# Four instead of three column groups of an input projection begin with the first half of their rows

## The chip, the cores and the metric

One core of one Trainium2 chip runs the whole program in one launch. The metric is the device time of that launch in microseconds (us), and lower is better. The engines are named as the profile names them: PE (TensorE, the matrix products; PEld is its weight load), DVE (VectorE), ACT (ScalarE), POOL (GpSimd) and SP (SyncE, which here issues the large loads).

## What is computed

Two transformer blocks over 256 tokens of width 2048, in float32. What matters here is the first half of the first block, and the keys and values of the second block's memory attention, which need nothing of the first block and are computed ahead.

```python
def first_block(x, c, w_ada, b_ada, norm1_w, w_in, ...):
    cond = jax.nn.silu(c)
    mod = cond @ w_ada[i] + b_ada[i]                      # 12288 columns
    shift1, scale1, gate1, shift2, scale2, gate2 = jnp.split(mod, N_MOD, axis=-1)
    h = _modulate(_rms(x, norm1_w[i]), shift1, scale1)
    proj = h @ w_in[i]                                    # 2048 x 4096
    u, q, k, v = jnp.split(proj, splits, axis=-1)
    y_ssm = _s5_mixer(u, ...)                             # a state-space scan, then gelu and a gate (w_glu)
    y_att = _dilated_attention(q, k, v, q_norm_w[i], k_norm_w[i])
    mixed = jnp.concatenate([y_ssm, y_att], axis=-1) @ w_out[i]
    x = x + gate1[:, None, :] * mixed
    ...
# of the second block, over the memory mem:
    k = (mem_n @ w_k)
    v = (mem_n @ w_v)
```

## The kernel before

**Weight tiles.** Every large product runs over weight tiles of 512 rows and 512 columns (1 MB), loaded by SP into six buffers `r` in the order of one list, `W`. A tile of kind "w" is split by `split_half` in two halves of 256 rows, each into a rounded part `h` (ACT, line 207) and a rest `l` (DVE, line 208), and `mm3` multiplies them on PE in three passes (lines 221, 222 and 226) into a PSUM tile `g` of two banks for the 256 tokens. There are four buffers for the halves, so ACT and DVE can be two tiles ahead of PE. A tile of kind "a" carries 128 x 2048 of `w_ada`; it meets no product, DVE sums it against `cond` in one instruction (line 964), eight such sums make half of one of the six modulation vectors.

**Column groups.** `group` takes the tiles of one group of 512 columns, one per block of 512 rows, and hands the finished PSUM tile to a function (`done_u`, `done_q`, `done_k`, `done_v`). The input projection `w_in` has eight groups: u0, u1, q2, q3, k4, k5, v6, v7. A group in the list `EARLY` is taken in two parts: rows 0 to 1023 first, whose sum `hold` copies to SBUF by ACT (line 891), and later rows 1024 to 2047, after which `tok` adds the held sum on DVE (line 887) where otherwise it would copy by ACT.

**Order.** Below, w0, w1, ... are the "w" tiles in the order of the list. Stage A is w0 to w37: 16 tiles for the memory's keys, 16 for its values, and the first halves of u0, u1 and q2 (w32 to w37), with 32 ada tiles spread among them by `mixed`, which leaves the last tiles of a stage without. These 32 sums give shift1 and scale1: the first 16 of them the columns of row blocks 0 and 1, the rest those of 2 and 3, without which the second halves can't start. Stage B is w38 to w83: the second halves of u0, u1 and q2 (w38 to w43), then k4 (w44 to w47), v6, v7, q3, k5 (to w63), `w_out` row block 2 (w64 to w67), `w_glu` (w68 to w71), `w_out` row blocks 3 (w72 to w75) and 0 and 1 (w76 to w83), with 48 ada tiles spread among all but the last three.

**What runs beside.** Everything else is a set of Python generators that advance by one step for each "w" tile (`Flow.step`): the state-space sections (`Ssm.prep` and `Ssm.run`, eight sections, mostly DVE, which start when u0 is there), the attention heads (`head1`, in two sets of four), the gate vectors. Each engine then executes its instructions strictly in the order in which they were emitted. Where a product needs an input that isn't there yet, `Flow.until` advances the generators without a tile between: `w_glu` needs `glu_acts`, that is all eight sections, and `w_out` row block 3 needs heads 4 to 7 (the lists `mixed_acts`).

The 43 or 40 buffers of the class constant `NU` are SBUF buffers of 2 KB in each partition for all these intermediates.

Of the kernel before, what the change touches and what calls it, by code (L numbers as in the profile page):

```python
# [148 lines left out]


class Core:
    NU = 40
    NU2 = 15
    NR, NW = 6, 4

# [26 lines left out]
    def unit(self, shape=(128, 512), dtype=F32):  # L182
        return self.up.tile(list(shape), dtype, name=self.nm("u"), tag="u", bufs=self.NU)

# [257 lines left out]
class Ssm:  # L442
# [18 lines left out]
    def params(self):  # L461
# [5 lines left out]
        tmp = lambda: k.small(32)  # L467
        wide = lambda: k.up.tile([128, NA * 32], F32, name=k.nm("q"), tag="u", bufs=k.NU)

# [302 lines left out]
def build(ctx, tc, A, out):  # L772
    nc = tc.nc
    V, S, G, PE, SY = nc.vector, nc.scalar, nc.gpsimd, nc.tensor, nc.sync
    ctx.enter_context(tc.manual_schedule())
    k = Core(ctx, tc)
# [22 lines left out]
    def tiles(name, g, kbs):  # L799
        return [("w", A[name][g, kb]) for kb in kbs]  # L800

    def ada_tiles(*halves):
        return [("a", A["w_ada"][h, kb]) for h in halves for kb in range(8)]

    def mixed(ws, as_, lag=0, lead=0):

        n, m = len(ws) - lag - lead, len(as_)
        j = 0
        for i, w in enumerate(ws):
            W.append(w)  # L810
            while j < m and j * n < (i + 1 - lead) * m:
                W.append(as_[j])
                j += 1
        W.extend(as_[j:])

    R4 = range(4)
    EARLY = (("u", 0), ("u", 1), ("q", 2), )
    ADA = (8, 9, 6, 4, 5, 7)
    LATE = (("k", 4), ("v", 6), ("v", 7), ("q", 3), ("k", 5), )
    mixed(sum([tiles("w_xk", g, R4) for g in R4] + [tiles("w_xv", g, R4) for g in R4]  # L820
              + [tiles("w_in", g, (0, 1)) for _, g in EARLY], []), ada_tiles(2, 0, 3, 1), 3, LEAD)
    mixed(sum([tiles("w_in", g, (2, 3)) for _, g in EARLY]
              + [tiles("w_in", g, R4) for _, g in LATE], [])
          + sum([tiles("w_out", g, (2,)) for g in R4], [])
# [37 lines left out]
    def group(acts, done, kbs, key=None, first=True, last=True, half=None):  # L862


        ps = open_ps.pop(key) if not first else [k.pm(), k.pm()] if half else k.pg()
        for i, kb in enumerate(kbs):
            parts = yield
            fl.until(lambda: kb in acts)
            end = last and i == len(kbs) - 1
            for ts in ((0,), (1,)) if half and end else ((0, 1),):  # L870
                for j in range(2):
                    k.mm3(ps, acts[kb][2 * j:2 * j + 2], parts[j], first and i == 0 and j == 0,
                          end and j == 1, ts)
                if half and end:
                    half(ps[ts[0]], ts[0])
        if half:
            return
        if last:
            fl.add(done(ps))
        else:  # L880
            open_ps[key] = ps
# [151 lines left out]
    def hold(g):  # L1033
        def done(ps):
            held[g] = tok(ps)
            yield
        return done
# [518 lines left out]
    def main():  # L1556
# [14 lines left out]
        done = {"u": done_u, "q": done_q, "k": done_k, "v": done_v}  # L1571
        for n, g in EARLY:
            yield from group(acts1, hold((n, g % 2)), (0, 1))
        for n, g in EARLY:
            yield from group(acts1, done[n](g % 2), (2, 3))
        for n, g in LATE:
            yield from group(acts1, done[n](g % 2), R4)
# [77 lines left out]
```

## Time and profile before

| | us |
|---|---|
| median of three runs | 2687.2 |
| lowest and highest run | 2685.88, 2689.08 |
| the profiled execution | 2691.46 |
| its span in the trace | 2689.7 |
| busy in the span: PE, DVE, ACT, POOL | 2609.1, 1663.0, 1270.9, 101.0 |

The page divides the span into 40 slices of 67 us. The part up to about 650 us, the first ten, is stage A, stage B and a little more. There the slices of DVE read 7997999987 and those of PE 8899998988; behind it PE reads 9 in every slice but the last and DVE 4 to 7. A reader finds in the timeline of an engine the rows in order of time, with the wait before an instruction in brackets and what ended it; tiles can be counted there by line 208, two instructions for each.

### The profile page before, as it was taken

How to read it: one execution, taken by the hardware profiler on the slowest of the kernel's cores; microseconds unless marked ns; L12 is line 12 of the kernel's file. 1: busy time of each engine (PE TensorE's matmuls, PEld its weight loads, DVE VectorE, ACT ScalarE, POOL GpSimd, SP SyncE). 2: the span in 40 equal slices, each digit the busy share in tenths (PEclk: the TensorE clock that was granted, in tenths of full speed). 3: DMA queues.
4: the chain of work that ended last, by engine and by line, in shares of the span. 5: the costliest groups of instructions: out<-in, count | busy, mean ns of one | idle time of the engine just before them, and what ended most of it. 6: DMA issues, size and time to landing. Idle time of an engine off the chain costs nothing.

```text
span 2689.7 us, 31097 instructions
## 1 busy us (share of the span) xinstructions
PE 2609.1 (97%) x12144; PEld 2164.5 (80%) x12144; DVE 1663.0 (62%) x2016; ACT 1270.9 (47%) x1818; POOL 101.0 (4%) x107
## 2 busy tenths in 40 slices
PE   8899998988999999999999999999999999999998
PEld 6678777867888888888888788888888888888887
DVE  7997999987766544554565445655554554554444
ACT  5366456654544344434455555555544434443443
POOL 3000000100000000000000111000000000000001
PEclk9999999998999999999999999999999999999999
DMA  9988765776766555555446434455555555555552
GB/s 356 352 328 319 304 235 216 287 281 231 289 266 238 193 198 188 192 199 188 184 152 219 153 130 171 165 196 184 179 205 194 188 192 188 188 188 191 188 201 94
DMA packets 90147, 578.98 MB, mean 215 GB/s; under 512 B 10000, under 2 KB 12432, under 8 KB 22672
## 3 DMA queue, kind: packets, MB, share of 16 engines
q1 hardware_dynamic: 80928, 561.61, 56.2%
q10 hardware_dynamic: 9072, 15.38, 1.7%
q8 instruction: 95, 1.56, 0.2%
q14 instruction: 52, 0.43, 0.0%
HBM read 570.67 MB, written 6.29 MB: 215 GB/s over the span
## 4 chain that ended last, share of the span: by engine, by line
PE 80%; DVE 14%; ACT 3%; issue 2%; DMA 1%; POOL 0%; ACTq 0%; DVEq 0%; POOLq 0%
PE g L226 25%; PE g L221 25%; PE g L222 24%; DVE l L208 4%; DVE r L964 4%; PE m L238 2%; DVE v L645 1%; ACT h L207 1%; PE m L345 0%; PE m L1504 0%; PE m L1491 0%; PE m L240 0%; DVE C L653 0%; DMA r<-in_w_ada_dram 0%; PE m L226 0%
## 5 line engine op out<-in xcount | busy, mean ns | idle before, releaser
L208 DVE TENSOR_TENSOR l<-r,h 128x1024 fp32r<-128x1024 f32 x866 | 1028.5, 1223 | 569.4 <-ACT h L207 564.4
L221 PE MATMUL g<-h,u 128*128 128x512 f32 x3424 | 1352.5, 395 | 8.2 <-ACT h L207 5.0
L222 PE MATMUL g<-h,u 128*128 128x512 f32 x3424 | 1336.6, 390 | 0.0
L207 ACT ACTIVATE h<-r 128x1024 fp32r<-128x1024 f32 x866 | 883.7, 1056 | 613.7 <-PE g L222 574.5
L226 PE MATMUL g<-l,u 128*128 128x512 f32 x3424 | 920.9, 391 | 34.8 <-DVE l L208 34.8
L226 PEld LDWEIGHTS g<-l,u 128*128 128x128 f32 x3424 | 641.6, 188 | 181.0 <-DVE l L208 49.2
L221 PEld LDWEIGHTS g<-h,u 128*128 128x128 f32 x3424 | 646.7, 189 | 146.0 <-ACT h L207 9.2
L222 PEld LDWEIGHTS g<-h,u 128*128 128x128 f32 x3424 | 646.7, 189 | 132.6 <-issue 1.9
L964 DVE CUSTOM_DVE_ANT_0 r<-r,cond,vec 128x2048 f32<-128x2048 f32 x96 | 224.5, 2343 | 0.2
L274 ACT ACTIVATE u<-m 128x512 fp32r<-128x512 f32 (+1 forms) x80 | 42.8, 575 | 162.4 <-PE m L238 130.9
L294 ACT ACTIVATE j<-u 128x512 bf16<-128x512 f32 (+2 forms) x92 | 47.3, 514 | 120.5 <-DVE u L1224 33.2
L275 DVE TENSOR_TENSOR u<-m,u 128x512 fp32r<-128x512 f32 (+1 forms) x80 | 50.0, 659 | 80.5 <-ACT u L274 80.4
L277 ACT ACTIVATE u<-m,vec 128x256 fp32r<-128x256 f32 x86 | 38.9, 472 | 69.8 <-PE m L345 30.8
L278 DVE SCALAR_TENSOR_TENSOR u<-m,vec,u 128x256 fp32r<-128x256 f32 x86 | 40.0, 481 | 46.5 <-ACT u L277 46.5
L238 PE MATMUL m<-ident,u 128*128 128x128 f32 x372 | 51.7, 283 | 13.1 <-DMA u<-in_mem_dram 8.8
L238 PEld LDWEIGHTS m<-ident,u 128*128 128x128 f32 x372 | 44.9, 146 | 19.8 <-issue 9.4
L302 POOL TENSOR_TENSOR r<-s,mhalf 128x2 f32<-128x2 f32 x5 | 5.5, 1103 | 1084.3 <-DVE s L301 1084.3
L1255 DVE SCALAR_TENSOR_TENSOR w<-g,r,w 128x512 f32<-128x512 f32 x22 | 15.5, 747 | 44.4 <-PE g L226 44.4
L1271 DVE TENSOR_TENSOR w<-g,w 128x512 f32<-128x512 f32 x24 | 16.5, 688 | 40.8 <-PE g L226 40.8
L1527 DVE TENSOR_TENSOR u<-g,u 128x512 f32<-128x512 f32 x22 | 14.2, 686 | 44.3 <-PE g L226 44.3
L1253 DVE TENSOR_TENSOR w<-g,w 128x512 f32<-128x512 f32 x22 | 14.2, 686 | 44.3 <-PE g L226 44.3
L1247 ACT ACTIVATE w<-g,r 128x512 f32<-128x512 f32 x22 | 13.9, 686 | 52.9 <-PE g L226 52.9
(244 smaller groups left out, 1198.0 us busy)
## 6 DMA issues: line engine op xcount, KB each, us to landing
r<-in_w_ada_dram SPq DMA_DIRECT2D x96, 1024.0 KB, 5.7
r<-in_wg_dram SPq DMA_DIRECT2D x88, 1024.0 KB, 4.8
r<-in_wu_dram SPq DMA_DIRECT2D x88, 1024.0 KB, 4.8
r<-in_wd_dram SPq DMA_DIRECT2D x88, 1024.0 KB, 4.8
r<-in_w_in_dram SPq DMA_DIRECT2D x32, 1024.0 KB, 5.8
r<-in_w_out_dram SPq DMA_DIRECT2D x32, 1024.0 KB, 4.9
r<-in_w_qkv_dram SPq DMA_DIRECT2D x24, 1024.0 KB, 4.8
r<-in_w_xk_dram SPq DMA_DIRECT2D x16, 1024.0 KB, 8.0
```

The source lines that it names most:

```text
L207: nc.scalar.activation(h, r, AF.Copy)
L208: (nc.gpsimd if shared else nc.vector).tensor_tensor(l, r, h.bitcast(F32), op=OP.subtract)
L221: nc.tensor.matmul(ps[t][:, :n], al[:, s], h[:, k], start=first and k == 0, stop=False)
L222: nc.tensor.matmul(ps[t][:, :n], ah[:, s], h[:, k], start=False, stop=False)
L226: nc.tensor.matmul(ps[t][:, :n], ah[:, s], l[:, k], start=False, stop=last and k == len(acts) - 1)
L238: self.nc.tensor.transpose(o, i, self.ident)
L274: nc.scalar.activation(h, ps, AF.Copy)
L275: nc.vector.tensor_tensor(l, ps, h.bitcast(F32), op=OP.subtract)
L277: nc.scalar.activation(h, ps, AF.Copy, scale=w)
L278: nc.vector.scalar_tensor_tensor(l, ps, w, h.bitcast(F32), op0=OP.mult, op1=OP.subtract)
L294: self.nc.scalar.activation(j[:, :n], src, AF.Square, accum_out=acc)
L964: V.tensor_tensor_reduce(r, r, cond, 1.0, v("b_ada", 8 * h + j), OP.mult, OP.add, md[h // 2][:, n:n + 1])
```

## The change

```diff
 class Core:
-    NU = 40
+    NU = 43
...
-    EARLY = (("u", 0), ("u", 1), ("q", 2), )
+    EARLY = (("u", 0), ("u", 1), ("q", 2), ("k", 4))
     ADA = (8, 9, 6, 4, 5, 7)
-    LATE = (("k", 4), ("v", 6), ("v", 7), ("q", 3), ("k", 5), )
+    LATE = (("v", 6), ("v", 7), ("q", 3), ("k", 5), )
...
-    nc = bacc.Bacc("TRN2", target_bir_lowering=False, num_devices=1, dynamic_dma_scratch_size=512)
+    nc = bacc.Bacc("TRN2", target_bir_lowering=False, num_devices=1, dynamic_dma_scratch_size=128)
```

The group k4 joins `EARLY`. Its first two tiles become w38 and w39, the last of stage A, and their sum is held in SBUF; the second halves of u0, u1, q2 and k4 follow as w40 to w47. From w48 on every weight tile has its old place. Stage A has 40 tiles instead of 38 for the same 32 ada tiles, stage B 44 instead of 46 for 48. Three buffers are added to the 40 and the reserve for DMA descriptors shrinks, to make room for the held sum.

In the following excerpts of the engines' orders, `l`, `h` and `r` are the parts and the load of a weight tile, `g` and `m` PSUM tiles, `u` intermediates; a line of "..." marks rows that are left out.

DVE, from tile w34 on, before: the last sum of stage A (L964) stands just above this, and L267 finishes the modulated input of row block 2.

```order
L208 TENSOR_TENSOR l_2144<-r_2057,h_2143 128x1024
L208 TENSOR_TENSOR l_2148<-r_2057,h_2147 128x1024
L208 TENSOR_TENSOR l_2183<-r_2060,h_2182 128x1024
...
L208 TENSOR_TENSOR l_2217<-r_2099,h_2216 128x1024
...
L267 TENSOR_TENSOR u_2255<-u_2256,u_2254 128x512
```

DVE, from tile w34 on, after:

```order
L208 TENSOR_TENSOR l_2138<-r_2051,h_2137 128x1024
L208 TENSOR_TENSOR l_2142<-r_2051,h_2141 128x1024
L964 ISA r_2054,mod_111<-r_2054,cond,vec 128x2048
...
L208 TENSOR_TENSOR l_2180<-r_2093,h_2179 128x1024
...
L964 ISA r_2096,mod_111<-r_2096,cond,vec 128x2048
...
L208 TENSOR_TENSOR l_2217<-r_2132,h_2216 128x1024
```

The last two sums of stage A moved behind w34 and w35, and L267 comes two tiles later; of the sums, 24 now stand before w28 where it was 26.

PE, between the last tile of `w_out` row block 2 (w67) and the first of `w_glu` (w68), before: eight transposes of the first glu input, eight of the second, and the scores of head 4 (L1105).

```order
L226 MATMUL g_4593<-l_4566,u_3992 128x512 x4
L238 MATMUL m_4646<-ident,u_2542 128x128
...
L238 MATMUL m_4664<-ident,u_3497 128x128
...
L1105 MATMUL m_4682<-u_4543,u_4186 128x128
...
L221 MATMUL g_4645<-h_4613,u_4652 128x512
```

PE, in the same place, after (L757 is the output of the last state-space section, L1105 the scores of a head, L1121 the transposes of head 4, L980 a gate vector):

```order
L226 MATMUL g_4574<-l_4547,u_3933 128x512 x4
L757 MATMUL m_4623<-u_2747,u_4344 128x64
...
L1105 MATMUL m_4638<-u_4524,u_4092 128x128
...
L1105 MATMUL m_4681<-u_4524,u_4092 128x128
...
L238 MATMUL m_4700<-ident,u_2615 128x128
...
L1121 MATMUL m_4736<-ident,u_4644 128x128 x3
L1105 MATMUL m_4745<-u_4531,u_4099 128x128
...
L980 MATMUL m_4760<-u_4653,ones 128x512
L221 MATMUL g_4622<-h_4590,u_4706 128x512
```

The last section's output moved from the place before w66 to this one, and three heads are scored here where it was one: two steps of the generators are run off without a tile between.

PE, between w71 (the last of `w_glu`) and w72 (the first of `w_out` row block 3), before: the outputs of heads 5, 6 and 7 (L1127), with transposes between.

```order
L1127 MATMUL m_4959<-u_4885,u_3709 128x128
...
L1121 MATMUL m_4965<-ident,u_4817 128x128 x3
L1127 MATMUL m_4996<-u_4969,u_3709 128x128
...
L1121 MATMUL m_5004<-ident,u_4896 128x128 x3
L238 MATMUL m_5010<-ident,u_4974 128x128
...
L1127 MATMUL m_5028<-u_5008,u_3709 128x128
...
L221 MATMUL g_4958<-h_4926,u_4878 128x512
```

PE, in the same place, after:

```order
L226 MATMUL g_4862<-l_4894,u_3732 128x512 x4
L1127 MATMUL m_4991<-u_4933,u_3647 128x128
L1128 MATMUL m_4991<-u_4933,u_3647 128x128
L1129 MATMUL m_4991<-u_4933,u_3648 128x128
L221 MATMUL g_4990<-h_4958,u_4793 128x512
```

Only the output of head 7 is left here; the other steps went ahead of w68.

## Rows read from the trace of the kernel before

**Rows 1.** Stretches: us; then PE, PEld, DVE, ACT, POOL busy; granted clock, DMA share, GB/s.

```profile
80.00:100.00 20.00, 16.71 (x75) 13.28 (x76) 19.55 (x59) 6.11 (x8) 0.53 (x1) 1.00 1.00 364
...
220.00:240.00 20.00, 20.00 (x90) 16.55 (x89) 15.21 (x14) 9.97 (x12) 0.00 (x0) 1.00 1.01 426
...
560.00:580.00 20.00, 13.15 (x52) 9.73 (x53) 14.96 (x20) 12.32 (x25) 0.00 (x0) 0.74 0.70 260
```

**Rows 2.** Timeline of PE, w28 to w30: start, duration, instruction, wait and its releaser.

```profile
206.06 1.20 PE L226 MATMUL g<-l,u 128*128 128x512 f32 x4 [0.35 <-DVE l L208]
...
211.63 1.07 PE L226 MATMUL g<-l,u 128*128 128x512 f32 x4
...
217.07 1.07 PE L226 MATMUL g<-l,u 128*128 128x512 f32 x4
```

**Rows 3.** Timeline of DVE: w28, a sum, w29, w33, w35 and w36, w39.

```profile
204.78 2.36 DVE L208 TENSOR_TENSOR l<-r,h 128x1024 fp32r<-128x1024 f32 x2
207.06 2.35 DVE L964 CUSTOM_DVE_ANT_0 r<-r,cond,vec 128x2048 f32<-128x2048 f32 x1
...
209.33 2.36 DVE L208 TENSOR_TENSOR l<-r,h 128x1024 fp32r<-128x1024 f32 x2
...
228.59 2.36 DVE L208 TENSOR_TENSOR l<-r,h 128x1024 fp32r<-128x1024 f32 x2 [1.00 <-ACT h L207]
...
239.28 4.79 DVE L208 TENSOR_TENSOR l<-r,h 128x1024 fp32r<-128x1024 f32 x4 [3.79 <-ACT h L207]
...
269.43 2.35 DVE L208 TENSOR_TENSOR l<-r,h 128x1024 fp32r<-128x1024 f32 x2
```

**Rows 4.** Timeline of DVE: a sum before w26, and the wait before w28.

```profile
190.09 2.35 DVE L964 CUSTOM_DVE_ANT_0 r<-r,cond,vec 128x2048 f32<-128x2048 f32 x1
...
200.00 0.69 DVE L267 TENSOR_TENSOR u<-u,u 128x512 fp32r<-128x512 f32 x1 [0.75 <-ACT u L265]
```

**Rows 5.** Timeline of DVE in stage B, up to w67.

```profile
276.29 1.29 DVE L887 TENSOR_TENSOR u<-g,u 128x512 f32<-128x512 f32 x2
...
288.92 0.69 DVE L739 TENSOR_TENSOR u<-m,u 128x512 f32<-128x512 f32 x1 [1.49 <-PE m L736]
...
493.94 0.69 DVE L739 TENSOR_TENSOR u<-m,u 128x512 f32<-128x512 f32 x1 [1.21 <-PE m L736]
...
508.88 0.68 DVE L750 TENSOR_TENSOR u<-u,u 128x512 f32<-128x512 f32 x1
...
510.88 2.35 DVE L964 CUSTOM_DVE_ANT_0 r<-r,cond,vec 128x2048 f32<-128x2048 f32 x1
...
517.95 2.36 DVE L208 TENSOR_TENSOR l<-r,h 128x1024 fp32r<-128x1024 f32 x2 [0.17 <-ACT h L207]
```

**Rows 6.** Timeline of DVE from w68 to w73: the waits, and the first head.

```profile
527.35 2.48 DVE L275 TENSOR_TENSOR u<-m,u 128x512 fp32r<-128x512 f32 x4 [2.08 <-ACT u L274]
529.75 0.34 DVE L1110 SCALAR_TENSOR_TENSOR u<-m,rq,u 128x128 f32<-128x128 f32 x1
...
535.01 2.36 DVE L208 TENSOR_TENSOR l<-r,h 128x1024 fp32r<-128x1024 f32 x2 [1.48 <-ACT h L207]
...
547.95 1.29 DVE L1183 TENSOR_TENSOR u<-u,u 128x512 f32<-128x512 f32 x2 [3.05 <-ACT u L1182]
...
557.90 1.29 DVE L275 TENSOR_TENSOR u<-m,u 128x512 fp32r<-128x512 f32 x2 [2.29 <-ACT u L274]
...
566.97 1.29 DVE L1183 TENSOR_TENSOR u<-u,u 128x512 f32<-128x512 f32 x2 [2.84 <-ACT u L1182]
...
579.15 1.29 DVE L1205 TENSOR_TENSOR u<-g,u 128x512 f32<-128x512 f32 x2 [2.20 <-PE g L226]
```

**Rows 7.** Timeline of PE between w71 and w72: the waits.

```profile
560.95 0.49 PE L1127 MATMUL m<-u,u 128*128 128x128 f32 x2 [2.82 <-ACT u L1123]
...
564.68 1.09 PE L1121 MATMUL m<-ident,u 128*128 128x128 f32 x3 [2.80 <-ACT u L1117]
...
567.81 2.27 PE L238 MATMUL m<-ident,u 128*128 128x128 f32 x8 [2.04 <-DVE u L1183]
```

## The prediction

> **What bounds the kernel now.** [...]
>
> Read second, the two engines' rows at the end of stage A [rows 2, 3]. PE takes 5.44 us for a weight tile (217.07 less 211.63, both the same block of two tiles in a row). DVE takes 2.27 us for the two `l` halves of a tile and 2.27 us for a sum over an ada tile, 4.55 us for the pair (209.33 less 204.78). While DVE also has the state-space preparation it is the slower one: PE waits for its `l` until w28 (206.06, released by DVE). From w28 PE is the slower one, and at 228.59 and 239.28 DVE waits for an `h` whose buffer PE still holds.
>
> Read third, the waits of DVE before w_glu and w_out [rows 6] and of PE in the same place [rows 7].
>
> **The change part by part.** From w48 on every tile stands where it stood; k4's first two tiles move from w44 and w45 to w38 and w39, and the six tiles of u0, u1 and q2 come two tiles later. The 32 sums of stage A spread over 35 tiles, not 33, the 48 of stage B over 41, not 43.
>
> *Added work.* hold() copies k4's half sum out of PSUM (two copies on ACT), and done_k then adds on DVE where it copied on ACT. ACT has as many copies as before; DVE has two additions more, 1.29 us by the same addition for u (the row of 276.29) [rows 5]. No other engine gains an instruction; the buffers (43) and the scratch change no row. **+1.3 us**.
>
> *End of stage A.* By the order 24 sums stand before w28, not 26. One of the two was taken out early (w14), where DVE decides: 2.27 us gained. The other stood at 190.09 [rows 4]; behind it DVE waits 0.75 us for ACT at 200.00 anyway, and PE's own transposes set the rest, so I count 2.1. At w28 the changed kernel is thus 4.4 us ahead. From there PE sets the pace, and there are two tiles more to the handover: 2 x 5.44 = 10.9 us. The handover, the first tile behind stage B's two leading sums (w39 at 269.43 [rows 3], now w41), comes 10.9 - 4.4 = 6.5 us later, near 275.9. DVE has done two tiles (4 x 1.14 = 4.55 us) more by then and equally many sums (34), so 6.5 - 4.55 = **1.95 us** of the delay is new idle time. Bounds: 1.8 (both sums count in full) to 4.5 (the transfers, below). The tiles and sums moved out of stage B are paid back there, since DVE decides.
>
> *Stage B up to w67.* From 269.43 to 517.95 [rows 3, 5] DVE idles 5.8 us in seven waits (1.49 at 288.92 the first, 0.17 at 517.95 the last) [rows 5]. The state-space sections run two tiles later, all in the same relation to their tiles. I take **0**, with bounds of 4.2 us on either side: the three waits of L739 for PE (1.49 us the first, 1.21 the last, 4.2 in sum) gone, or doubled. One thing stays behind: section 7's last four multiplications (2.00 us, 508.88 to 510.88 [rows 5]) stand after w65 now and after w67 then.
>
> *The forced steps.* w68 needs all eight sections, w72 needs heads 4 to 7, and what is not ready is run off without a tile between. The order shows two such steps of the heads before w72 and none before w68; after the change two before w68 (section 7 is late) and none before w72. Before: from 520 to 580 us DVE idles in six gaps [rows 6], 2.08 + 1.48 + 3.05 + 2.29 + 2.84 + 2.20 = 13.9 us; the last three lie at w72, where PE waits 2.82 + 2.80 + 2.04 [rows 7]. After, walked along the order from the end of w67's `l`, with the durations of the same instructions: DVE reaches head 4 at 7.4, and w69's `l` starts 5.3 us later as it did (529.75 to 535.01), a gap of 2.1; behind head 5 the copies of the glu inputs come on ACT after its exp and four gate copies, a gap of 2.8; DVE then stands before head 4's output, which waits for PE to do all of w68 (5.44 us) and the product, a gap of 5.7 and a small one of 0.4; then one of 2.8 for the sigmoid with its table load. That is 13.8, **-0.1 us**. Bounds: -7.3 if the three gaps at w72 go and nothing new comes (2.29 + 2.84 + 2.20), +7.3 if they come twice.
>
> *Sum.* 1.3 + 1.95 + 0 - 0.1 = +3.1 us. It is made against the profiled execution, 2691.46 us (span 2689.7 and 1.8 around it): 2694.6. That execution is 4.3 us above the median of the runs, 2687.2, and the same difference there gives **2690.3 us**. About 0.2% (5.4 us) is what a measurement of this kernel can tell from no change, so this counts as no change.
>
> **Rivals.** *The forced steps cost more at w_glu than they did at w_out (slower).* For it: before w68 they need DVE, which still has sums and tiles queued ahead of the last section's transposes, and ACT, where the exps and gate copies stand ahead of the glu copies; at w72 they mostly needed ACT and PE; and a longer gap of PE lowers its clock behind it, as in 560 to 580 [rows 1]. Against it: PE has 8 us of small work there to cover them. Price: the gaps at w72 twice, 7.3 us, 2690.3 + 7.3 = 2697.6. In my walk PE idles 11 us between w67 and w68; the rival decides from about 14 (2.4 us more take the sum past 5.4).
>
> *They are covered (faster).* In the kernel before, the glu transposes and a score run between w67 and w68 and DVE waits only 2.08 us. If the new ones hide as well, the gaps at w72 go, and the one for the sigmoid (3.05) too, since heads no longer crowd ACT there: 7.3 + 3.05 = 10.4 us less, 2679.9. Against it: w68 cannot start before a chain over DVE, PE, ACT and DVE again.
>
> *The transfers fall behind at the end of stage A (slower).* From w28 to w35 each tile now has its sum: 16 transfers of 1.05 MB in 8 x 5.44 = 43.5 us, 385 GB/s. The stretch 80 to 100 with DMA fully busy moved 364 GB/s, 220 to 240 moved 426 [rows 1]. At 364 the 16.8 MB take 46.1 us: 2.6 more, 2692.9, just beyond what counts as the same. [...] Hence a small chance.
>
> That the change does not do what it says is ruled out by the order.
>
> **How the numbers follow.** The likeliest case is the walk, within 5.4 us of 2687.2: 0.56. The forced steps dearer: 0.22. The transfers: 0.08. Covered: 0.14. So slower 0.30, same 0.56, faster 0.14. The range goes up to the dear forced steps, 2697.6, rounded to 2698, and down to 2682: the sum with the lower bounds of stage A and of the forced steps (2690.3 - 0.15 - 7.3 = 2682.9) and a little of stage B's waits. Left out are the covered case and the far ends of stage B added to others, under 2 in 10.
>
> **What would show it.** Stage A: w41's `l` on DVE near 276, w39's near 265 (tiles at PE's 5.44 us in between), DVE's idle time between 200 and 276 some 2 us longer; if w28 to w35 show DVE or ACT waiting for r<-in_w_ada or r<-in_w_in, the transfers were too slow. Stage B: eight L887 additions, not six, and w67's `l` ending within 2 us of 520.2. Forced steps: PE idle 11 us before w68, next to none before w72; the sum of DVE's gaps from w67 to w73 between 11 and 17 us. A gap above 17, or w73's `l` more than 5 us late, is the slower rival; under 7, the faster one. Wrong altogether would be a difference that first appears behind w78, where the order is the same.

## The result and the profile after

Four executions of the changed kernel gave a median of 2702.61 us (2701.54 to 2703.36), the kernel before beside them 2688.04 us; the ratio is 1.0055, interval 1.0043 to 1.0067. The change makes the kernel slower by 14.6 us where I forecast 3.1 and called that no change; 2702.6 lies above the range. The profiled execution took 2702.5 us, so here profile and median agree.

The page of the changed kernel (span 2700.7 us), each engine's busy time:

```profile
PE 2609.9 (97%) x12144; PEld 2168.5 (80%) x12144; DVE 1664.0 (62%) x2018; ACT 1268.2 (47%) x1816; POOL 100.6 (4%) x107
```

The page tells little: DVE has 2 instructions more than before (2016), and the shares stand. The stretches tell more. First the kernel before, from the start to the handover (w39's `l`), on to w67's, to w74's and to w92's; then the changed kernel with the same tiles, its handover being w41 (columns: stretch, its length, DVE's busy time and instructions, granted clock, DMA share, GB/s):

```profile
0.00:269.43 269.43, 227.95 (x364) 1.00 0.89 338
269.43:517.95 248.52, 240.28 (x389) 0.97 0.68 256
517.95:582.63 64.68, 50.45 (x71) 0.92 0.73 277
582.63:701.50 118.87, 96.98 (x111) 0.94 0.70 267
sum 701.50, DVE 615.67; mean DVE 153.92
```

```profile
0.00:276.69 276.69, 232.71 (x368) 1.00 0.88 337
276.69:525.72 249.03, 232.55 (x381) 0.94 0.65 244
525.72:593.73 68.01, 52.48 (x77) 0.92 0.66 249
593.73:712.35 118.62, 99.05 (x113) 0.94 0.73 282
sum 712.35, DVE 616.79; mean DVE 154.20
```

Length less busy time is DVE's idle time, and the sum of the prediction can be read off term by term:

| | idle before | idle after | difference | forecast |
|---|---|---|---|---|
| to the handover | 41.48 | 43.98 | +2.50 | +1.95 |
| handover to w67 | 8.24 | 16.48 | **+8.24** | 0 |
| w67 to w74 | 14.23 | 15.53 | +1.30 | -0.1 |
| w74 to w92 | 21.89 | 19.57 | -2.32 | 0 |
| DVE's work, 616.79 - 615.67 | | | +1.12 | +1.3 |
| sum, 712.35 - 701.50 | | | +10.85 | +3.1 |

The 8.24 us are the miss. What DVE waited for from the handover to w67, before and then after (total us, times, longest):

```profile
DVE u L739 <- PE m L736: 4.2, 3, 1.5
DVE l L208 <- ACT h L207: 1.0, 3, 0.5
DVE s L301 <- ACT j L294: 0.6, 1, 0.6
```

```profile
DVE u L739 <- PE m L736: 8.2, 3, 3.9
DVE s L301 <- ACT j L294: 4.4, 2, 3.0
DVE l L208 <- ACT h L207: 1.5, 1, 1.5
```

Two things grew: L301 (the head norm's first step, which needs ACT's eight squares L294) by 3.8 us, and L739 (a state-space addition that needs PE's L736) by 4.0. **L301**, DVE's timeline around the ends of q2 and k4 after the change (rows of L887 and L301 only):

```profile
319.32 1.25 DVE L887 TENSOR_TENSOR u<-g,u 128x512 f32<-128x512 f32 x2
328.59 0.17 DVE L301 TENSOR_SCALAR s<-s 128x8 f32<-128x8 f32 x1 [1.41 <-ACT j L294]
336.97 1.25 DVE L887 TENSOR_TENSOR u<-g,u 128x512 f32<-128x512 f32 x2
341.19 0.17 DVE L301 TENSOR_SCALAR s<-s 128x8 f32<-128x8 f32 x1 [2.97 <-ACT j L294]
```

k4's two additions end at 338.22 and the very next instruction of DVE needs the squares of their result. In the kernel before ACT copied k4 itself (from ACT's timeline, first row), squared it, and DVE came to its L301 (from DVE's, second row) with state-space work up to that point and no wait:

```profile
341.22 1.09 ACT L891 ACTIVATE u<-g 128x512 f32<-128x512 f32 x2
346.89 0.16 DVE L301 TENSOR_SCALAR s<-s 128x8 f32<-128x8 f32 x1
```

q2's wait of 1.41 us is of another kind. DVE added q2's halves in the kernel before, too, with the same rows between the additions and L301, and did not wait. Now ACT comes late to q2's squares, because a step ahead of them in its order waits for PE:

```profile
323.51 0.38 ACT L763 ACTIVATE y<-m 128x256 f32<-128x256 f32 x1 [12.79 <-PE m L759]
```

PE is late there in the way that is shown next: two sums behind w45 left it idle for 3.62 us, and its granted clock was 0.72 from 314.4 to 324 us. No run tests this place by itself, but in e2 (below), whose first edit lies behind it, the clock was 0.82 from 313.4 to 323 us and q2's wait 0.49 us.

**L739**, the last and worst of the three. DVE's timeline has two sums in a row before w64's `l` (500.27), and L739 later:

```profile
495.75 2.32 DVE L964 CUSTOM_DVE_ANT_0 r<-r,cond,vec 128x2048 f32<-128x2048 f32 x1
...
498.00 2.35 DVE L964 CUSTOM_DVE_ANT_0 r<-r,cond,vec 128x2048 f32<-128x2048 f32 x1
...
515.40 0.69 DVE L739 TENSOR_TENSOR u<-m,u 128x512 f32<-128x512 f32 x1 [3.94 <-PE m L736]
```

PE's timeline has the last `h` matmul, the wait for that `l`, and what follows:

```profile
495.49 0.39 PE L222 MATMUL g<-h,u 128*128 128x512 f32 x1
501.54 2.07 PE L226 MATMUL g<-l,u 128*128 128x512 f32 x4 [5.67 <-DVE l L208]
503.42 0.63 PE L221 MATMUL g<-h,u 128*128 128x512 f32 x1
```

PE stands idle 5.67 us, and behind that a matmul of 512 columns takes 0.63 us instead of 0.39. The stretches of the wait and of what follows (length, PE's busy time, granted clock, DMA share, GB/s):

```profile
494.00:501.00 7.00, 1.88 (x9) 0.98 0.46 162
501.00:508.00 7.00, 6.46 (x16) 0.53 0.92 375
```

The granted clock was 0.98 in the wait and 0.53 behind it. PE's backlog then holds up L736, and DVE, which had made PE wait, waits for PE. The same stands at w52 (two sums in a row, PE idle 5.89 us, L739 2.77 us where it was 1.52). The two sums in a row are the spread's: 48 sums over 41 tiles give a second one behind w40, 45, 51, 57, 63, 69 and 75, 48 over 43 gave it behind w38, 46, 55, 63 and 72. So at w52 the second sum is new. Behind w63 two sums stood in the kernel before, too, and PE waited only 0.51 us for the `l` after them (DVE's rows of the two sums):

```profile
495.94 2.35 DVE L964 CUSTOM_DVE_ANT_0 r<-r,cond,vec 128x2048 f32<-128x2048 f32 x1
498.21 2.35 DVE L964 CUSTOM_DVE_ANT_0 r<-r,cond,vec 128x2048 f32<-128x2048 f32 x1
```

What is new at w64 is the long state-space step ahead of the two sums (490.89 to 495.75 in the changed kernel), which came two tiles earlier before.

### The profile page after: what moved, and what is told of

Its sections match the earlier page's. It is cut to its first block, busy times and chain, and to the rows that moved or that the text cites. A ratio compares the mean times of both kernels' runs of the same rounds, so it can differ in the third digit from the quotient of the medians.

```text
span 2700.7 us, 31088 instructions
## 1 busy us (share of the span) xinstructions
PE 2609.9 (97%) x12144; PEld 2168.5 (80%) x12144; DVE 1664.0 (62%) x2018; ACT 1268.2 (47%) x1816; POOL 100.6 (4%) x107
## 4 chain that ended last, share of the span: by engine, by line
PE 81%; DVE 14%; ACT 2%; issue 2%; DMA 1%; POOL 0%; DVEq 0%; ACTq 0%; POOLq 0%
PE g L226 25%; PE g L221 25%; PE g L222 25%; DVE l L208 4%; DVE r L964 4%; PE m L238 2%; DVE v L645 1%; ACT h L207 0%; PE m L345 0%; DVE C L653 0%; PE m L1504 0%; PE m L1491 0%; ACT j L294 0%; PE m L240 0%; DVE X L653 0%
## 5 line engine op out<-in xcount | busy, mean ns | idle before, releaser
L964 DVE CUSTOM_DVE_ANT_0 r<-r,cond,vec 128x2048 f32<-128x2048 f32 x96 | 224.4, 2343 | 0.2
L294 ACT ACTIVATE j<-u 128x512 bf16<-128x512 f32 (+2 forms) x92 | 47.3, 514 | 109.1 <-DVE u L1272 26.3
L1253 DVE TENSOR_TENSOR w<-g,w 128x512 f32<-128x512 f32 x22 | 14.2, 685 | 44.3 <-PE g L226 44.3
L1527 DVE TENSOR_TENSOR u<-g,u 128x512 f32<-128x512 f32 x22 | 14.2, 686 | 44.3 <-PE g L226 44.3
```

The costliest lines, as they stand in the source:

```text
L294: self.nc.scalar.activation(j[:, :n], src, AF.Square, accum_out=acc)
L964: V.tensor_tensor_reduce(r, r, cond, 1.0, v("b_ada", 8 * h + j), OP.mult, OP.add, md[h // 2][:, n:n + 1])
```

## The experiments

Theory A: L301's waits are a direct price of the change (I took it for q2 and k4 alike; by the rows above it can hold for k4 only). Theory C: two sums in a row on top of a long state-space step let PE run dry, its clock falls, and L739 waits. The first four start from the changed kernel.

**L301 one step later (e1).**

```diff
             o = tok(ps, base=held.pop(("k", g), None))
-            r = heads_rstd(o)
+            ss = heads_ss(o)
+            if g == 0:
+                yield
+            r = k.rstd(ss, 8, 128.0)
             yield
```

(`heads_ss` is `heads_rstd` without its last line; done_q has the same edit.)

> The changed kernel with one yield more in done_q and done_k of the two groups whose first half is held (q2, k4): the eight squares on ACT are issued as before, and L301 on DVE comes one step later, behind the next tile's l. Theory A (the waits that L301 brought, 1.41 us for q2 and 2.97 us for k4, are a direct cost of the change, since DVE now adds k4's halves itself and stands before the squares that follow on ACT): both waits go, 4.4 us off, about 2698 where the changed kernel took 2702.6. Rival B (DVE's next wait for PE grows by what this one gives back): 2702 to 2703, with a longer wait at L739 or L208.

2697.03 us (ratio to before 1.0034, 1.0021 to 1.0047), 5.6 less. DVE's waits from the handover to w67:

```profile
DVE u L739 <- PE m L736: 5.6, 2, 3.6
DVE l L208 <- ACT h L207: 3.1, 2, 1.7
```

L301 is gone from the list. Of the 4.4 us, 1.66 came back as a wait of w49's `l` for ACT, whose split of that tile stands behind the squares: A holds with 2.7 us, B with the rest. The two late waits of L739 are 1.1 us shorter in sum. Another 1.49 us less is not the edit's: the first L739 did not wait here at all, though up to there both kernels issue the same instructions (last section).

**The two sums moved (e2).** A loop over the list of tiles, behind the two calls of `mixed`, moves one sum each:

```diff
+    move(51, 49)
+    move(63, 66)
```

> The changed kernel with two sums of stage B at other places: the second of the two behind w51 goes behind w49, the second of the two behind w63 goes behind w66. No work is added or left out. Theory C (two sums in a row on top of a long state-space step keep PE waiting 5.9 and 5.7 us for l, its clock falls to half behind each, and L736 is late for DVE's L739): PE's gaps there fall to about 3.5 us, the granted clock stays 1.0 in 370 to 385 and 495 to 510, the two waits of L739 fall from 2.77 and 3.94 to about 1.5 and 1.2 us, 4 us off: about 2698.6. Rival D (the waits of L739 follow from the sections' standing two tiles later, wherever the sums are): 2702 to 2703, L739 waits 6 us or more in its two later places.

2697.22 us (1.0035, 1.0022 to 1.0047).

```profile
DVE s L301 <- ACT j L294: 3.5, 2, 3.0
DVE u L739 <- PE m L736: 2.8, 1, 2.8
```

L739 fell from 8.2 to 2.8 us (1.49 of it the first wait, which is missing here as in e1) though the sections stand where they stood, which goes against D: what counts is that a long step and two sums meet. Behind w52 the wait is gone; PE's clock fell all the same, but earlier, where the sum went (0.77 from 360 to 375). Ahead of w64 PE still waited 3.41 us, its clock fell less (0.76 from 494 to 501), and 2.75 of 3.94 us are left.

**Both (e3).**

> Both edits, the later L301 and the two moved sums. If A and C hold and the two costs add: 4.4 + 4.0 = 8.4 us off, about 2694.2, which leaves 6 us over the kernel before (1.1 of added work, 2.5 at the handover, the rest at the forced steps and in the pairing with the runs of before). If the waits only move (B, D): over 2700.

2695.19 us (1.0023, 1.0012 to 1.0034). Profile against profile, w92's `l` comes 7.4 us earlier than in the changed kernel; 5.9 and 5.7 with the single edits, each with the 1.49 us that are not theirs and that this one hasn't. Without them it is 4.4 + 4.3 against 7.4: the edits add but for 1.3 us. In part this is q2's L301, which had lost 0.9 of its 1.41 us in e2 ahead of that edit.

**Filler for PE: is it the clock (e4)?**

```diff
             fl.until(lambda: kb in acts)
+            if fl.nth in (53, 65) and i == 0:
+                for _ in range(22):
+                    PE.matmul(ps[:, 0], acts[kb][0][1][:, 0:128], parts[0][0][:, 0], start=True, stop=True)
```

> The changed kernel with 22 matmuls of 128x512 more (5 us at 0.23 us each) on PE ahead of the first matmul of w52 and of w64, in whose place it stood idle; their sum is overwritten, so nothing else changes, and DVE and ACT have their order of before. Theory C (it is the clock): PE's l matmuls start when they did, at full clock, the two waits of L739 fall to about 1.5 and 1.2 us, 4 us off although PE does 10 us more: about 2698.6. Rival E (PE is late because l is late, whatever its clock): nothing gained, 2702 to 2704.

2697.45 us (1.0035, 1.0021 to 1.0048): 44 matmuls more, 5.2 us less. PE's stretches around w64, then DVE's waits:

```profile
490.00:497.00 7.00, 7.00 (x32) 1.00 0.44 159
497.00:504.00 7.00, 7.00 (x43) 1.00 0.88 362
```

```profile
DVE u L739 <- PE m L736: 1.8, 1, 1.8
```

The two sums stand in a row as they did, and the `l` of w52 and w64 come as long behind the `l` ahead of them as they did (11.6 and 11.7 us). L739's two late waits are down by 2.8 and 2.2 us; the first is missing here too, ahead of any filler. Rival E falls: it is the clock. This is the experiment that shows the mechanism; the moved sums only show where it starts.

**Buffers alone (e5), and another group (e6).** The kernel before with `NU = 43` and the scratch of 128, and the changed kernel with v6 in k4's place:

```diff
-    EARLY = (("u", 0), ("u", 1), ("q", 2), ("k", 4))
+    EARLY = (("u", 0), ("u", 1), ("q", 2), ("v", 6))
-    LATE = (("v", 6), ("v", 7), ("q", 3), ("k", 5), )
+    LATE = (("k", 4), ("v", 7), ("q", 3), ("k", 5), )
```

> The kernel before with 43 buffers and the smaller DMA scratch, its order of instructions unchanged. All theories: no change (2686 to 2690); its profile is also a second look at the order of before, which tells how much of the idle time in the first is always there: L739's waits of 1.49 and 1.52 us may be absent where the clock does not fall at 272 and 361.

> Four groups ahead as in the changed kernel, but v6 in k4's place (v6 has no squares and no L301 behind its additions; k4 then runs whole behind them, copied by ACT). Theory A (k4's L301 stands straight behind additions that are now DVE's own): the wait of 2.97 us at w48 is gone, 1.3 to 3 us off (1.3 if ACT's squares hold up the next tile as they did with the later L301), 2699.5 to 2701.5. Theory C (doubles at w52 and w64 and the clock) is untouched by it: L739's waits there stay at 5 us or more in sum. Rival (which group is taken makes no difference): 2702 to 2703.

Buffers: 2688.28 us (1.0002, 0.9993 to 1.0010), nothing; its profile repeats that of before to 0.5 us at every tile, with the same falls of the clock. v6: 2697.37 us (1.0033, 1.0021 to 1.0046), 2.1 us below the range that A gave. k4's wait of 2.97 us at L301 is gone, q2's is there (1.45), and L739 keeps 5.4 us (2.58 and 2.81 the longest), as A (for k4) and C say. The first L739 does not wait here either, which is 1.49 us of the surplus; the rest stays open.

**The same step for w_glu (e7, e8).** An attempt to carry e1's lesson to the kernel before: a yield in done_glu between ACT's sigmoid and DVE's product L1183.

> The kernel before with one yield more in done_glu, between ACT's sigmoid and DVE's product L1183, so that the next tile's l and sum stand between them. No work is added. If what held for L301 holds here too (an instruction that DVE issues right behind the one of ACT that it waits for costs the whole chain): the waits of 3.05 and 2.84 us at L1183 go, up to 5.9 us off, about 2682. Rival (w_out's first half waits for the product, and the wait moves there): 2687 to 2689.

2688.24 us (1.0000, 0.9991 to 1.0009): a miss, as the rival said. From w67 to w74 before, then with the edit (where L1205 is L1207):

```profile
DVE u L1183 <- ACT u L1182: 5.9, 2, 3.1
DVE u L275 <- ACT u L274: 4.4, 2, 2.3
DVE u L1205 <- PE g L226: 2.2, 1, 2.2
DVE l L208 <- ACT h L207: 1.7, 2, 1.5
```

```profile
DVE u L1207 <- PE g L226: 6.1, 1, 6.1
DVE u L275 <- ACT u L274: 4.9, 4, 2.1
DVE l L208 <- ACT h L207: 3.9, 3, 2.2
```

L1183 no longer waits, and the sum of the waits is what it was (14.2, now 14.9). As I read it, PE decides here, which w72 holds up in the forced steps, and DVE waits for it sooner or later. The same edit on top of both others:

> Four groups ahead with the later L301, the two moved sums and the yield in done_glu. If the costs add: 2695.2 (with the first two) less up to 5.9, about 2690; the four groups would then still stand 5 to 8 us behind three groups with the yield alone, since one more group ahead adds 1.1 us of DVE's work and 2.5 us at the handover and gives nothing back. Rival (with its waits gone, the larger number of groups wins): below e7.

2693.64 us (1.0020, 1.0011 to 1.0029), above the 2690 forecast, 5.4 behind e7, 1.5 under e3 and inside its spread. As e7 gave nothing, I count nothing for it here.

**Zeros for PE in the kernel before (e9 to e14).** If idle PE costs the clock, the kernel before pays too. Matmuls of zeros into a sum that is open (or not yet begun) change nothing in it:

```diff
+    def burn(self, n, o, start=True):
+        for _ in range(n):
+            self.nc.tensor.matmul(o, self.zf[:, 0:128], self.zf, start=start, stop=start)
...
+        self.burn(idle, ps[0][:, :n], False)
...
+        k.burn(15, k.pg()[:, 0])
         fl.add(norm2())
```

The first two: 10 in w39 and 11 in w50 between the `h` and the `l` matmuls; 15 ahead of norm2. The third has all and 10 at w72. The fourth starts from e3, with 52 in w41, w46, w51, w52 and w64 and 15 ahead of norm2.

> The kernel before with matmuls of zeros (128x512, 0.23 us each, added to the open sum, so nothing changes in it) on PE where it waits for l ahead of a fall of its clock: 10 in w39 (gap 2.37 us) and 11 in w50 (2.70 us). If idle PE is what makes the clock fall, the falls at 272 and 361 are gone and with them L739's waits of 1.49 and 1.52 us: up to 3.0 us off against an execution that has both falls, 1 to 3 us in the medians, 2685 to 2687, and a mean granted clock no longer at 0.990. Rival (the falls come on a schedule of their own): falls and waits as before, 2687.5.

> The kernel before with 15 matmuls of zeros ahead of norm2's 32 (L240, 655.01 to 661.73, 6.72 us at the lower clock), where PE stands idle 3.82 us. Behind this PE is full to the end, so here the clock itself is the price: at full clock the 32 take about half, 3.4 us off, about 2684. Rival (ACT's scaling behind L240 sets the time, or the fall moves elsewhere): within 1 us of 2687.5.

> The kernel before with the zeros of both and 10 more at w72's first forced step (gap 2.82 us). If the places add: 3.4 us for norm2, 1 to 3 for the sums, 0 to 3 at w72 (the clock's 0.74 of 560 to 580 went with waits of DVE for PE of 2.2 us): 2680 to 2683. Rival: the slack is taken by ACT's chains, 2685 to 2688.

> Four groups ahead with the later L301 and the two moved sums, and zeros in w41, w46, w51, w52 and w64 (10, 15, 12, 8, 7) and ahead of norm2 (15). Same theory: 3.4 us for norm2 and 1 to 3 for the falls that stage B still has, from 2695.2 to about 2689 to 2691, still over three groups with the zeros by the 1.1 us of added work, the 2.5 us at the handover and the forced steps. Rival (the fourth group pays once the clock is out of it): below e11.

2692.33, 2692.98, 2690.55 and 2695.52 us (1.0016, 1.0018, 1.0009 and 1.0025): none met its forecast, and the three from the kernel before came out slower than it, by my own doing. The tile of zeros was made by ACT as its first work, ahead of the first loads that it issues, and the first `l` came at 18.8 to 20.6 us where it comes at 12.79. By w86 most of that was made good, but the times can't tell by what. With the tile made late in stage A:

> Three groups ahead, as e11 (zeros in w39 and w50, at w72's first forced step and ahead of norm2), the tile of zeros made by ACT behind the memory's values instead of at the start. In e11 7.8 us went at the start and 7.6 us came back by w86; with the start as before about 7 us are left against an execution with all falls, 4 to 5 in the medians: 2682.5 to 2684. Rival (what came back in e11 was only the later start's slack): 2687 to 2689.

> Four groups ahead with the later L301, the two moved sums and the zeros of e12, the tile of zeros made late. From e12's 2695.5 less 6.7 at the start: about 2689. If the fourth group has a price of its own (1.1 us of additions, 2.5 to 3 us at the handover, about 1 at the forced steps, where this kernel's clock still falls): 4 to 6 us over e13. If the falls of the clock were all of it: level with e13.

Three groups with the zeros: **2684.79 us** (0.9987, 0.9978 to 0.9996), 0.8 above its forecast and clear of the rival, the fastest kernel of this study. The falls behind w39 and w50 are gone (granted clock 1.00 from 268 to 278 and from 360 to 372, where the kernel before had 0.83 and 0.86), and so are L739's first two waits. At w72 the ten matmuls gave nothing: the clock fell to 0.62 from 562 to 570, and w67 to w74 took 64.87 us where it took 64.68. Four groups with zeros: 2691.83 us (1.0012, 1.0003 to 1.0021), 7.0 us behind, more than the 4 to 6 forecast. norm2's 32 matmuls behind PE's idle 3.82 us before, and in e13 (L249 there), where the zeros fill it:

```profile
655.01 6.72 PE L240 MATMUL m<-w,u 128*128 128x128 f32 x32 [3.82 <-DVE w L1233]
```

```profile
649.61 3.84 PE L249 MATMUL m<-w,u 128*128 128x128 f32 x32 [0.38 <-DVE w L1248]
```

The granted clock was 0.58 from 653 to 661 in the first and 1.00 from 648 to 656 in the second: 2.9 us less for the same work. In e14 L301 waits nowhere and L739 1.1 us in all, and w92's `l` is still 7.2 us behind e13's: 1.4 of more work, 2.9 of idle time up to the handover (0.4 of it at the very start), 2.1 from there to w67, and 0.8 behind it. The work and the idle time up to the handover without the start, 3.9 us, came at a granted clock of 1.00 in both kernels: this is the price of the fourth group itself. In the other 2.9 us e14's clock was still the lower one (0.96 for 0.98 up to w67, 0.90 for 0.95 up to w74, 0.97 for 1.00 behind), so they are not shown to be free of it.

## Why the prediction was wrong

*The bound.* The forecast counts DVE's work and idle time up to w78, with [rows 1, 2, 3] as the reason to take DVE for the engine that decides. DVE's work and idle time up to w92 give 10.85 of the 11.0 us between the spans, and behind w92 nothing is lost or won. That length is work plus idle time is bookkeeping and tests nothing; that nothing changes behind w78 did not hold (below).

*Added work.* Right: 1.12 us for 1.3, eight L887 where there were six.

*End of stage A.* Right, a little short: the handover came at 276.69 (275.9 forecast), 3.65 us ahead at w28 (4.4 forecast; the wait of 0.75 us [rows 4] grew to 1.30), 2.50 us of new idle time (1.95). The transfers did not fall behind: 423 GB/s from 220 to 240, as 426 in [rows 1], and every wait of an `l` there was for an `h`. Both rates are over the 364 GB/s at which I had worked out the price of that rival.

*Stage B: the step that failed.* "The state-space sections run two tiles later, all in the same relation to their tiles. I take 0", with bounds of 4.2: 8.24 came. Two terms were missing. First, I had written that hold() makes DVE add where ACT copied and priced only the addition; who reads the sum next, and what stands between on DVE's queue, I did not ask. It was k4's L301, with nothing between: 2.97 us. Second, I spread the sums as a count per stage and looked at their number before a tile, not at pairs: the sections kept their relation to their tiles, but not to the sums. Long steps and two sums met at w52 and w64, PE ran dry for 5.9 and 5.7 us, and its clock fell (0.55 from 375 to 382, 0.53 from 501 to 508). (By its rows q2's 1.41 us belongs here too.) [rows 1] showed such a fall at 560, and I used it only for the forced steps. L739's waits [rows 5] I did bound, by "gone, or doubled": they doubled, 4.2 to 8.2. The bound held, and the value 0 inside it was a choice without a reason from the order. The 3.8 us more at L301 then carried the sum out of the bound.

*The forced steps.* Right. After, on DVE from w68 to w71:

```profile
536.14 0.35 DVE L1110 SCALAR_TENSOR_TENSOR u<-m,rq,u 128x128 f32<-128x128 f32 x1 [1.54 <-issue]
541.40 2.36 DVE L208 TENSOR_TENSOR l<-r,h 128x1024 fp32r<-128x1024 f32 x2 [1.48 <-ACT h L207]
547.96 2.48 DVE L275 TENSOR_TENSOR u<-m,u 128x512 fp32r<-128x512 f32 x4 [2.31 <-ACT u L274]
550.98 0.35 DVE L1110 SCALAR_TENSOR_TENSOR u<-m,rq,u 128x128 f32<-128x128 f32 x1 [0.47 <-PE m L1106]
558.95 0.42 DVE L275 TENSOR_TENSOR u<-m,u 128x256 fp32r<-128x256 f32 x1 [6.45 <-ACT u L274]
571.16 1.29 DVE L1183 TENSOR_TENSOR u<-u,u 128x512 f32<-128x512 f32 x2 [2.84 <-ACT u L1182]
```

15.1 us (13.8 forecast), and PE idle 7.23 + 2.35 = 9.6 (11 forecast) before w68, nothing at w72. Against [rows 6, 7] the waits moved and nearly kept their sum; with the small gaps it is +1.3 us. Neither the dear nor the covered rival came; the time was slower by another mechanism than the one I held against my forecast. One of my signs of the dear rival misled: w73's `l` came 14.1 us late, but 7.8 of these stood at w67 already.

*Behind w74.* 2.3 us came back, all of it behind w80, where the order is the same; I had excluded that. The clock fell in other places there than before (0.91 from 612 to 622, 0.75 to 632 and 0.66 from 652 to 662 in the kernel before; 0.83 from 613 to 623 and from 633 to 643, and 0.66 from 663 to 673 in the changed one); no run tests that this is the reason.

*From the profile to the median: the second failure.* I took 4.3 us off because the profiled execution of before lay so far over its median. That is a matter of the clock, too: of 27 executions of the kernel before beside e5 to e8, 20 at a mean granted clock of 0.992 or 0.993 have a median of 2687.4, seven at 0.990 or 0.991 of 2691.3, and the profiled one was at 0.991. All four of the changed kernel stood at 0.988, so nothing was to be taken off. This is read off the executions' clocks; no run tests it. 2702.6 less 2690.3 is 12.3 us: 7.9 from the sum (2702.5 for 2694.6) and 4.4 from this. Without stage B's 8.24 us the kernel would have come at about 2694.4, inside the range in spite of the second failure.

Open: why executions of one kernel differ in it, what the last 2 us of the fourth group's price in stage B are (1.66 of them is probably the `l` that waits behind the squares, which no run took away), and how much of the price is still the clock.

## What to carry to other kernels

When a step moves from one engine to another, price not only the step but the instruction that reads its result: find it on its queue and see what stands between. When work is spread evenly over a list, look at where two pieces fall together, and what stands on that tile already; a mean says nothing of it. And look for the clock in the profile behind every long wait of PE, and at who then waits for the slowed PE: in e2 the granted clock was 0.77 from 360 to 375 and the wait of L739 behind w52 was gone, in the changed kernel it was 0.53 from 501 to 508 and L739 waited 3.94 us.

## What the runs showed of the hardware that was not expected

Matmuls that compute nothing made a kernel faster: 44 of them took 5.2 us off the changed kernel (5.0 by its two late waits of L739), and 46 took 2.6 us off the kernel before. Where they filled waits of 2.4 to 5.9 us the granted clock stayed at 1.00, except at w72 (0.62), where waits of 2.80 and 2.04 us followed that they did not fill. In e4 PE was busy all of the 7 us from 490 to 497, and the granted clock from 497 to 504 was 1.00; in the changed kernel it was busy 1.88 of the 7 us from 494 to 501, and the clock from 501 to 508 was 0.53.

The same wait does not always cost the clock. At the handover PE waited 2.38 us in the changed kernel and 2.37 us in e1, at the same instruction; the stretch 276 to 286 then had

```profile
276.00:286.00 10.00, 8.03 (x28) 0.83 0.97 383
```

in the first and

```profile
276.00:286.00 10.00, 7.63 (x34) 1.00 1.00 385
```

in the second, and with it L739's first wait was 1.49 us or none. Why is open: one trace of each kernel was kept, and up to there the two issue the same instructions. Such a chance of 1.5 us is half of what I had forecast for the whole change. A profile of one execution therefore can't place an effect of this size, and two edits can only be compared place by place, as in e1 to e3.
